# A transformer block on one core: x2's tiles turned into operands stage by stage, low parts of weights emitted later, gate's first sums on VectorE

## The chip, the core and the metric

The kernel runs on one core of one Trainium2 chip. The metric is the device time of one execution in microseconds (us); of several runs the median counts. The engines are named as in the profile: PE (TensorE) multiplies matrices, DVE (VectorE), ACT (ScalarE) and POOL (GpSimd) work on elements, and SP (SyncE) issues the large transfers. Each engine works through its own instructions in the order in which the program emits them, and waits on semaphores for the others. So the order of emission is the schedule.

## The reference, cut to what is computed

One layer of a hybrid decoder block on 512 tokens of width 2048, all in float32:

```python
h = _rms_norm(x, norm1_g)
aq, ak, av, bu, bg, cq, ck, cv = split(h @ w_in)
out_a = _dilated_mixture(rms(aq), rms(ak), av)          # 8 heads x 64, three dilations
out_b = _conformer_conv(bu, bg, conv_w, conv_b, ...)    # 512 channels, 31 taps
out_c = _band_attention(rms(cq), rms(ck), cv, 127, sinks)  # 16 query heads, 2 kv heads
x = x + concat(out_a, out_b, out_c) @ w_out             # "x2" in the kernel
h2 = _rms_norm(x, norm2_g)
x = x + (silu(h2 @ w_gate) * (h2 @ w_up)) @ w_down      # inner width 5632
```

## The kernel before

**Number format.** A float32 product is made of reduced-precision (fp32r) products: each operand is split into a high part, which is the rounded value, and a low part, which is the rest. `mm3` (L244 to L247) does high·high, high·low and low·high for each 128×128 block of weight against 512 tokens. The weight is the stationary operand, the activation the moving one. Activations lie transposed: features on partitions, tokens along the row.

**Weights.** Weights come in units of 128×1024. `pump` issues their loads on SP into raw buffers, `split_up_to` splits them: ScalarE copies the high part wh (L222), VectorE subtracts it for the low part wl (L223). In the FFN ScalarE writes a second copy of the high part, wn, into PSUM (L226), and VectorE subtracts from that (L228). A unit is split two units ahead of its use: `next_unit` emits the split of unit u + 2 and the loads at the start of unit u. There are three buffers each for wh and wl. Some FFN weight tiles are sums of others (`add`, L174, on GpSimd), named 's' and '21' below.

**Order around the change.** The schedule is written out by hand. `Ticks` is a queue: `ticks.after(n, fn, ...)` has fn emitted n ticks later. The projections (`project`) tick after every second of the eight k steps of a unit, the o-projection after every fourth, so a unit of 24 matmuls (eight k steps of three) has two ticks there. During the projections the attention and the convolution are emitted from these ticks, between the matmuls of the projections.

**The o-projection.** Two halves of the contraction, sixteen output tiles n each. Half 0 adds a tile of x to the partial sum (xr, L823) and keeps it in SBUF; half 1 adds the second partial sum (L826), which gives x2[n]. Half 1 goes through n in the order 0, 8, 1, 9, …, 7, 15, so that pairs (j, j + 8) follow one another. In `residual` x2[n] is stored to DRAM on SP, squared and summed into ssum2 for the norm (L343 on ScalarE, L344 on VectorE), and once both tiles of a pair are there `h2_of(j)` makes the operands of the FFN: two scalings (L808, ScalarE), four sums and differences of 256 columns (L813 to L816, VectorE) and seven operands, each a high part by ScalarE (L801) and a low part by VectorE (L802). All of that is emitted in one string at one tick.

**The FFN.** Gate and up products are done as 2×2 blocks with seven products instead of eight, over j = 0 … 7, in the order 5, 1, 7, 6, 2, 4, 3 (called q5, q1, and so on). Each is eight matmuls with high weights over 512 columns (operand's high and low part side by side) and eight with low weights over 256 columns (L916). The first group, g0, starts right after the o-projection. There, q5 and q1 are multiplied for j < 6 first (`EARLY`), then for j = 6 and 7, and then the norm's statistics follow (`norm2a`: matmuls L285, POOL power L352), and after the third product the spread of the norm over the partitions (`norm2b`: transposes L291, ScalarE copies r2b, L880 and L881), both in the bank of the fourth product. `evacs` hold the VectorE reads of a product's bank, emitted after the next product's start.

Of the kernel before, what the change touches and what calls it, by code (L numbers as in the profile page):

```python
# [15 lines left out]
P = 128  # L16
# [93 lines left out]
def kernel(ctx: ExitStack, tc: tile.TileContext, xT, wi, wo, wgu, wd, cst_in, outT):  # L110
# [19 lines left out]
    def slot(name, dt=F32, cols=T):  # L130
        return sp.tile([P, cols], dt, name=name, tag="s")
# [29 lines left out]
    def group(name, m, n, blocks):  # L161

        key = {k: (k, name) for k in ("11", "12", "21", "22", "s")}
        for k in ("21", "22", "11", "12"):
            entries.append((k + "ab"[m] if k == "22" else k, key[k], blocks[k]))
        u = len(works)

        def add(to, a, b, last=None):
            def go():
                if to == a:  # L170
                    out = raws[key[to]][0]
                else:
                    out = take("s" + "ab"[m], key[to], n)
                nc.gpsimd.tensor_add(out[:, :n], raws[key[a]][0][:, :n], raws[key[b]][0][:, :n])  # L174
                if last:
                    drop(key[last])
            return go

        sums[u - 4].append(add("s", "21", "22"))
        sums[u - 3].append(add("21", "21", "11"))  # L180
        sums[u].append(add("s", "s", "11", "11"))
        sums[u + 2].append(add("s", "s", "12"))
        works.extend((key[k], last, None) for k, last in (
            ("s", False), ("11", False), ("21", True), ("s", False), ("12", True), ("22", True), ("s", True)))
# [19 lines left out]
    def pump(limit):  # L204
        while at["entry"] < len(entries) and len(raws) < limit and entries[at["entry"]][0] not in held:
            buf, key, parts = entries[at["entry"]]
            t, o = take(buf, key, sum(p.shape[-1] for p in parts)), 0
            for part in parts:
                nc.sync.dma_start(t[:, o:o + part.shape[-1]], part)
                o += part.shape[-1]  # L210
            at["entry"] += 1

    def split_up_to(i):
        while at["split"] <= min(i, len(works) - 1):
            key, last, eng = works[at["split"]]
            t, n = drop(key) if last else raws[key]
            u = at["split"]
            hi = wp.tile([P, 1024], F32R, name=f"wh{u}", tag="hi", bufs=SPLIT_BUFS)
            lo = wp.tile([P, 1024], F32R, name=f"wl{u}", tag="lo", bufs=SPLIT_BUFS)
            if eng or "high" not in psum:  # L220
                eng = eng or nc.vector
                nc.scalar.copy(hi[:, :n], t[:, :n])  # L222
                eng.tensor_sub(lo[:, :n], t[:, :n], hi[:, :n].bitcast(F32))  # L223
            else:
                near = psum["high"].tile([P, 1024], F32R, name=f"wn{u}", tag="h")
                nc.scalar.copy(near[:, :n], t[:, :n])  # L226
                nc.scalar.copy(hi[:, :n], t[:, :n])
                nc.vector.tensor_sub(lo[:, :n], t[:, :n], near[:, :n].bitcast(F32))  # L228
            splits[u] = (hi, lo)
            at["split"] += 1  # L230
# [5 lines left out]
    def next_unit():  # L236
        sums_now()
        u = at["use"]
        at["use"] += 1
        split_up_to(u + SPLIT_AHEAD)  # L240
        pump(RAW_EARLY if u < 20 else RAW_BUFS)
        return splits.pop(u)

    def mm3(out, wh, wl, xh, xl, start, stop):  # L244
# [142 lines left out]
    def project(name):  # L387
        b = bank(name)
        for half in range(2):
            wh, wl = next_unit()  # L390
            for kk in range(8):
                k = 8 * half + kk
                s = slice(kk * P, (kk + 1) * P)
                mm3(b, wh[:, s], wl[:, s], h_hi[k], h_lo[k], k == 0, k == KT - 1)
                if kk % 2 == 1:
                    ticks.tick()
        return b
# [330 lines left out]
    def split_mix(name):  # L728
        if name not in m_hi:
# [3 lines left out]
            nc.vector.tensor_sub(lo, m, hi.bitcast(F32))  # L733
            m_hi[name], m_lo[name] = hi, lo

    ticks.after(1, spread_r1)
    ticks.after(2, glu, 0, g4[0], g4[1])
    ticks.after(2, glu, 1, g4[2], g4[3])
# [56 lines left out]
    def halves(t):  # L795
        return t[:, :TH], t[:, TH:]

    def operand(q, j, src):
        t = ops[q, j] = slot(f"h{q}_{j}", F32R)
        hi, lo = halves(t)  # L800
        nc.scalar.copy(hi, src)  # L801
        nc.vector.tensor_sub(lo, src, hi.bitcast(F32))  # L802

    def h2_of(j):
        h = []
        for n in (j, j + NJ):
            t = slot(f"h2_{n}")
            nc.scalar.activation(t, x2.pop(n), AF.Copy, scale=col(C_G2 + n))  # L808
            h.append(t)
        (h11, h12), (h21, h22) = halves(h[0]), halves(h[1])  # L810
        ta, tb = slot(f"ta{j}"), slot(f"tb{j}")
        (n1, n3), (n2, n4) = halves(ta), halves(tb)
        nc.vector.tensor_sub(n1, h11, h12)  # L813
        nc.vector.tensor_sub(n3, h12, h22)
        nc.vector.tensor_sub(n2, n3, h11)
        nc.vector.tensor_add(n4, n2, h21)  # L816
        for q, src in ((5, n1), (1, h11), (7, n3), (6, n2), (2, h21), (4, n4), (3, h22)):
            operand(q, j, src)

    def residual(n, b, half):  # L820
        if half == 0:
            t = x2[n] = xr.pop(n)
            nc.vector.tensor_add(t, t, b)  # L823
            return
        t = x2[n]
        nc.vector.tensor_add(t, t, b)  # L826
        nc.sync.dma_start(x2d[n], t)
        add_square(ssum2, t, n, "sr")
        if n >= NJ:
            h2_of(n - NJ)  # L830

    def split_rows(k):
        for name in ROWS[k:k + 3]:
# [6 lines left out]
    for half in range(2):  # L840
        for i, n in enumerate(OUT_ORDER[half]):
            if half == 1 and i == 2:
                ticks.drain()
                b = None
                open_banks(banks=4, high=2)
            b = bank(f"o{half}_{n}")
            wh, wl = next_unit()
            for kk in range(8):
                k = 8 * half + kk
                row = ROWS[k]  # L850
                while row not in m_hi and row not in mix:
                    ticks.tick()
                split_rows(k)
                s = slice(kk * P, (kk + 1) * P)
                mm3(b, wh[:, s], wl[:, s], m_hi[row], m_lo[row], kk == 0, kk == 7)
                if kk % 4 == 3 or i == 0:
                    ticks.tick()
            ticks.after(0, residual, n, b, half)
            if half == 0:
                load_x(i + 2)  # L860
        for row in ROWS[8 * half:8 * half + 8]:
            if half == 0:
                m_hi.pop(row), m_lo.pop(row)
    ticks.drain()
    m_hi = m_lo = r1b = mult_a = bias_a = bias_c = None

    r2b = cp.tile([P, 3 * TH], F32, name="r2b")
# [3 lines left out]
    outs = [bank(f"out{i}") for i in range(4)]  # L873

    def norm2a():
        n2["r"] = token_scale(ssum2, D, "n2", outs[3][:, :NT])[1]

    def norm2b():
        b = spread(n2["r"], "r2s", outs[3])
        nc.scalar.copy(R_12, b)  # L880
        nc.scalar.copy(r2b[:, T:], b[:, :TH])  # L881

# [14 lines left out]
    class Block:  # L897
# [6 lines left out]
            self.banks = dict(zip((5, 1, 7, 6), outs if m == 0 else (outs[3], outs[1], outs[2], outs[0])))  # L904
            self.banks.update({3: self.banks[5], 4: self.banks[7], 2: self.banks[1]})

        def multiply(self, q, w, xs, first=0, last=True):
            wh, wl = w
            b = self.banks[q]
            at = [(x, slice(j * P, (j + 1) * P)) for j, x in enumerate(xs, first)]  # L910

            begin = first == 0 and q in (5, 1, 6, 7)
            for low in ((0, 1) if flip[0] else (1, 0)):
                for x, s in at:
                    out, lhs, rhs = (b[:, TH:], wl, x[:, :TH]) if low else (b, wh, x)
                    nc.tensor.matmul(out, lhs[:, s], rhs, start=begin, stop=last and low == flip[0] and x is xs[-1],  # L916
                                     skip_group_check=True)
                    begin = False
            flip[0] = 1 - flip[0]
            if last:  # L920
                later(0, self.done, q)

        def both(self, q, out):
            nc.vector.tensor_reduce(out, self.banks[q].rearrange("p (a b) -> p b a", a=2),
# [141 lines left out]
            at = LAID.index(q)  # L1066
            nc.sync.dma_start(acts[q, j].bitcast(F32), od[j % NP][:, at * T:(at + 1) * T])

    EARLY = 6
    blk = gate = None  # L1070
    for g in range(2 * NP + len(DOWN)):
        t = g - 2 * NP
# [4 lines left out]
        else:  # L1077
            n, first, end = DOWN[t]
            blk = Down(t)
        early_w = []  # L1080
        for i, q in enumerate(ORDER):
            sums_now()
            run(evacs)
            w = next_unit()
            if g == 0 and i < 2:
                blk.multiply(q, w, [ops[q, j] for j in range(EARLY)], last=False)
                early_w.append((q, w))
                if i == 1:
                    for q, w in early_w:
                        blk.multiply(q, w, [ops[q, j] for j in range(EARLY, NJ)], EARLY)  # L1090
                    norm2a()
            elif t < 0:
                blk.multiply(q, w, [ops[q, j] for j in range(NJ)])
            else:
                blk.multiply(q, w, [acts[q, j] for j in range(first, end)])
            if g == 0 and i == 2:
                norm2b()

            if t == -1:
                for j in range(NJ):  # L1100
# [94 lines left out]
```

## Time and profile before

| what | us |
|---|---|
| median of 3 runs (lowest, highest) | 1935.17 (1934.69, 1935.21) |
| the profiled execution, whole | 1935.7 |
| its span in the trace | 1933.9 |
| PE busy in it | 1902.3 (98%) |
| DVE / ACT / POOL busy | 1471.1 / 1329.0 / 994.1 |
| mean granted TensorE clock | 0.992 |

The profile is of one execution. Its page begins with the busy time of each engine. A view of waits lists for what an engine waited: waiting line, releasing engine and line, microseconds in total, times, and the longest. The timeline lists instructions by start: start in us from the beginning of the span, duration, engine, line, operation, output and inputs, and in brackets the idle time of the engine before it and what ended that. Windows give the busy time of an engine in a stretch (length, busy time, number of instructions), then the TensorE clock that was granted (1.00 is full, 0.50 half), the share of DMA and GB/s. The projections with attention and convolution fill the span up to about 440 us, the o-projection 440 to 620, the FFN the rest.

### The profile page before, as it was taken

Reading aid. Unit: us, or ns where it says so; the run is one execution under the profiler, and the core shown is the slowest. Engines: PE = TensorE matmul, PEld = TensorE weight load, DVE = VectorE, ACT = ScalarE, POOL = GpSimd, SP = SyncE. Lnnn points to the kernel's source line nnn. Section 1 sums busy time; section 2 is a strip of 40 time slices with the busy share of each in tenths; the row PEclk is TensorE's granted clock in tenths of the full one; section 3 lists DMA queues with packets and bytes.
Section 4 is the critical chain, followed back from the end, with each engine's and each line's share of the span. In section 5 each row is a group of like instructions: output and inputs, shape, how many; then the busy total and the mean of one; then the engine's idle time right before and its main releaser. Section 6 shows DMA issues by size and latency. Waiting matters only on the chain.

```text
span 1933.9 us, 29230 instructions
## 1 busy us (share of the span) xinstructions
PE 1902.3 (98%) x10332; PEld 1645.4 (85%) x10332; DVE 1471.1 (76%) x2508; ACT 1329.0 (69%) x1782; POOL 994.1 (51%) x640
## 2 busy tenths in 40 slices
PE   8999999999999999999999999999999999999999
PEld 7888888778877888888888888888888788888888
DVE  6789998997468677777777777777777677767776
ACT  6355654553356888888888888888877577667675
POOL 0111011000001788877887888788876566656564
PEclk9999999989999999999999999999999899999999
DMA  7222222223342344444443544354538987777685
GB/s 263 80 100 67 66 89 75 72 86 115 120 127 80 120 158 165 147 148 169 154 157 135 181 141 171 127 181 145 172 128 294 363 277 277 269 242 272 202 278 194
DMA packets 125651, 319.48 MB, mean 165 GB/s; under 512 B 14016, under 2 KB 29504, under 8 KB 125504
## 3 DMA queue, kind: packets, MB, share of 16 engines
q1 hardware_dynamic: 125360, 317.51, 48.0%
q8 instruction: 81, 1.33, 0.3%
q14 instruction: 66, 0.54, 0.1%
q10 hardware_dynamic: 144, 0.10, 0.0%
HBM read 259.09 MB, written 57.15 MB: 164 GB/s over the span
## 4 chain that ended last, share of the span: by engine, by line
PE 69%; DVE 2%; DMA 1%; ACT 1%; issue 0%; DVEq 0%; SPq 0%; ACTq 0%
PE out L916 66%; PE o L246 1%; PE o L245 1%; DMA a<-od 1%; PE o L247 1%; DVE h L802 0%; DMA od<-u21st 0%; DVE xr L826 0%; DVE wl L223 0%; DVE ssum L344 0%; DVE ta L813 0%; ACT sr L343 0%; ACT h L808 0%; DVE wl L228 0%; ACT wh L222 0%
## 5 line engine op out<-in xcount | busy, mean ns | idle before, releaser
L916 PE MATMUL out<-h,wh 128*128 128x512 f32 x2464 | 590.7, 392 | 3.6 <-DVE h L802 3.6
L916 PEld LDWEIGHTS out<-h,wh 128*128 128x128 f32 x2464 | 454.1, 189 | 91.8 <-DVE h L802 4.1
L916 PEld LDWEIGHTS out<-h,wl 128*128 128x128 f32 x2464 | 316.6, 191 | 13.7 <-ACT r2b L881 1.2
L916 PE MATMUL out<-h,wl 128*128 128x256 f32 x2464 | 320.7, 283 | 1.2 <-ACT r2b L881 1.0
L916 PE MATMUL out<-a,wh 128*128 128x512 f32 x1232 | 300.0, 394 | 3.2 <-DMA a<-od 2.6
L916 PEld LDWEIGHTS out<-a,wh 128*128 128x128 f32 x1232 | 226.9, 189 | 50.5 <-DMA a<-od 3.7
L916 PEld LDWEIGHTS out<-a,wl 128*128 128x128 f32 x1232 | 160.9, 193 | 10.9 <-DMA a<-od 4.4
L916 PE MATMUL out<-a,wl 128*128 128x256 f32 x1232 | 164.8, 285 | 2.4 <-DMA a<-od 2.2
L222 ACT CAST wh<-w 128x1024 fp32r<-128x1024 f32 (+1 forms) x93 | 96.8, 1041 | 98.8 <-PE o L246 33.6
L223 DVE TENSOR_TENSOR wl<-w,wh 128x1024 fp32r<-128x1024 f32 (+1 forms) x93 | 112.5, 1210 | 63.9 <-ACT wh L222 63.6
L929 DVE TENSOR_TENSOR y<-y,out 128x256 f32<-128x256 f32 x120 | 50.6, 421 | 65.5 <-PE out L916 62.4
L422 DVE SCALAR_TENSOR_TENSOR y<-bu,cst,y 128x511 f32<-128x511 f32 (+14 forms) x120 | 87.6, 730 | 0.7
L174 POOL TENSOR_TENSOR w('s', 'g0')_5639<-w('21', 'g0')_5403,w('22', 'g0')_5439 128x1024 f32<-128x1024 f32 x1 | 2.4, 2403 | 116.2 <-DVE wl L223 116.2
L930 DVE TENSOR_TENSOR y<-y,out 128x256 f32<-128x256 f32 x120 | 50.5, 421 | 4.1
L246 PE MATMUL o<-ml_c,wh 128*128 128x512 f32 x128 | 51.0, 399 | 2.2 <-DVE ml_c L733 2.2
L245 PE MATMUL cq<-hh,wh 128*128 128x512 f32 x128 | 51.4, 401 | 1.4 <-DVE mix_c L701 1.4
L245 PE MATMUL o<-mh_c,wh 128*128 128x512 f32 x128 | 52.0, 407 | 0.0
L247 PE MATMUL o<-mh_c,wl 128*128 128x512 f32 x128 | 50.8, 397 | 0.0
L247 PE MATMUL cq<-hh,wl 128*128 128x512 f32 x128 | 50.0, 391 | 0.0
L246 PE MATMUL cq<-hl,wh 128*128 128x512 f32 x128 | 49.9, 390 | 0.0
L245 PE MATMUL in<-hh,wh 128*128 128x512 f32 x64 | 26.1, 408 | 5.2 <-ACT wh L222 5.2
L246 PEld LDWEIGHTS o<-ml_c,wh 128*128 128x128 f32 x128 | 24.6, 192 | 7.3 <-DVE ml_c L733 2.9
(3093 smaller groups left out, 4822.5 us busy)
## 6 DMA issues: line engine op xcount, KB each, us to landing
a<-od SPq DMA_DIRECT2D x196, 256.0 KB, 5.3
w<-in_wi SPq DMA_DIRECT2D x59, 512.0 KB, 3.6
w<-in_wo SPq DMA_DIRECT2D x32, 512.0 KB, 3.6
y<-x2d SPq DMA_DIRECT2D x48, 256.0 KB, 5.4
x2d<-y SPq DMA_DIRECT2D x64, 128.0 KB, 3.4
x<-in_xT SPq DMA_DIRECT2D x16, 256.0 KB, 7.2
xr<-in_xT SPq DMA_DIRECT2D x16, 256.0 KB, 3.9
x2d<-xr SPq DMA_DIRECT2D x16, 256.0 KB, 4.1
```

The costliest lines, as they stand in the source:

```text
L174: nc.gpsimd.tensor_add(out[:, :n], raws[key[a]][0][:, :n], raws[key[b]][0][:, :n])
L222: nc.scalar.copy(hi[:, :n], t[:, :n])
L223: eng.tensor_sub(lo[:, :n], t[:, :n], hi[:, :n].bitcast(F32))
L245: nc.tensor.matmul(out, wh, xh, start=start, stop=False)
L246: nc.tensor.matmul(out, wh, xl, start=False, stop=False)
L247: nc.tensor.matmul(out, wl, xh, start=False, stop=stop)
L422: nc.vector.scalar_tensor_tensor(yconv[j][:, i:], hconv[j][:, :T - i], c, yconv[j][:, i:], op0=ALU.mult, op1=ALU.add)
L916: nc.tensor.matmul(out, lhs[:, s], rhs, start=begin, stop=last and low == flip[0] and x is xs[-1], skip_group_check=True)
L929: sign(out, out if first is None else first, main)
L930: sign(out, out, rest)
```

## The change

Four things move; the arithmetic stays the same.

1. From the start of the attention (`late_lows`) to the end of the o-projection, the subtraction for a weight's low part and the loads by `pump` are emitted at the fourth k step of a unit instead of at its start, ahead of the tick there.
2. x2's tiles become operands in stages one tick apart: `residual`, then `scale_x2` (store and scaling), then `differences` and `square_x2`, then `high`, then `low`. q5's and q1's operands are made from the first tile of a pair alone, one stage ahead of the other five.
3. The early split of q5 and q1 goes: g0's products are multiplied whole. `norm2a` stands after the third product, `norm2b` after the fourth, each in a PSUM tile of the pool "high" that wn uses.
4. The four weight sums of the first gate group 'g0' are emitted on VectorE instead of GpSimd.

```diff
@@ in group(): add()
-                nc.gpsimd.tensor_add(out[:, :n], raws[key[a]][0][:, :n], raws[key[b]][0][:, :n])
+                eng = nc.vector if name == "g0" else nc.gpsimd
+                eng.tensor_add(out[:, :n], raws[key[a]][0][:, :n], raws[key[b]][0][:, :n])
@@ after pump()
+    lows, late_lows = [], []
+
+    def lows_now():
+        while lows:
+            fn, *args = lows.pop(0)
+            fn(*args)
+        if late_lows:
+            pump(RAW_EARLY if at["use"] <= 20 else RAW_BUFS)
@@ in split_up_to()
                 nc.scalar.copy(hi[:, :n], t[:, :n])
-                eng.tensor_sub(lo[:, :n], t[:, :n], hi[:, :n].bitcast(F32))
+                lows.append((eng.tensor_sub, lo[:, :n], t[:, :n], hi[:, :n].bitcast(F32)))
+                if not late_lows:
+                    lows_now()
@@ in next_unit()
+        lows_now()
         split_up_to(u + SPLIT_AHEAD)
-        pump(RAW_EARLY if u < 20 else RAW_BUFS)
+        if not lows:
+            pump(RAW_EARLY if u < 20 else RAW_BUFS)
@@ in project() and, ahead of "if kk % 4 == 3", in the o-projection
+                if kk == 3:
+                    lows_now()
                 if kk % 2 == 1:
                     ticks.tick()
@@ ahead of the attention
+    late_lows.append(True)
     ticks.after(1, spread_r1)
@@ operand(), h2_of() and the old residual() are replaced by
+    half_h = {}
+
+    def residual(n, b, half):
+        t = xr.pop(n) if half == 0 else x2[n]
+        nc.vector.tensor_add(t, t, b)
+        x2[n] = t
+        if half == 1:
+            ticks.after(1, scale_x2, n)
+
+    def scale_x2(n):
+        j = n % NJ
+        t = x2.pop(n)
+        nc.sync.dma_start(x2d[n], t)
+        h = slot(f"h2_{n}")
+        nc.scalar.activation(h, t, AF.Copy, scale=col(C_G2 + n))
+        half_h.setdefault(j, []).append(h)
+        ticks.after(1, differences, j, n)
+        ticks.after(1, square_x2, n, t)
+
+    def square_x2(n, t):
+        if n == 0:
+            nc.scalar.activation(ssum2, t, AF.Square)
+        else:
+            sq = slot(f"sr{n}")
+            nc.scalar.activation(sq, t, AF.Square)
+            ticks.after(1, nc.vector.tensor_add, ssum2, ssum2, sq)
+
+    def differences(j, n):
+        hs = half_h[j]
+        h11, h12 = halves(hs[0])
+        if n < NJ:
+            ta = slot(f"ta{j}")
+            n1, n3 = halves(ta)
+            hs.append(ta)
+            nc.vector.tensor_sub(n1, h11, h12)
+            ticks.after(1, high, j, ((5, n1), (1, h11)))
+            return
+        half_h.pop(j)
+        (n1, n3), (h21, h22) = halves(hs[1]), halves(hs[2])
+        n2, n4 = halves(slot(f"tb{j}"))
+        nc.vector.tensor_sub(n3, h12, h22)
+        nc.vector.tensor_sub(n2, n3, h11)
+        nc.vector.tensor_add(n4, n2, h21)
+        ticks.after(1, high, j, ((7, n3), (6, n2), (2, h21), (4, n4), (3, h22)))
+
+    def high(j, srcs):
+        for q, src in srcs:
+            ops[q, j] = slot(f"h{q}_{j}", F32R)
+            nc.scalar.copy(ops[q, j][:, :TH], src)
+        ticks.after(1, low, j, srcs)
+
+    def low(j, srcs):
+        for q, src in srcs:
+            hi, lo = halves(ops[q, j])
+            nc.vector.tensor_sub(lo, src, hi.bitcast(F32))
@@ after the o-projection
     ticks.drain()
+    lows_now()
+    late_lows.clear()
@@ norm2a, norm2b
-        n2["r"] = token_scale(ssum2, D, "n2", outs[3][:, :NT])[1]
+        b = psum["high"].tile([P, 1024], F32, name="n2b", tag="h")
+        n2["r"] = token_scale(ssum2, D, "n2", b[:, :NT])[1]
-        b = spread(n2["r"], "r2s", outs[3])
+        b = psum["high"].tile([P, 1024], F32, name="r2s", tag="h")[:, :T]
+        spread(n2["r"], "r2s", b)
@@ in the loop over products (multiply() loses its arguments first and last)
-            if g == 0 and i < 2:
-                blk.multiply(q, w, [ops[q, j] for j in range(EARLY)], last=False)
-                early_w.append((q, w))
-                if i == 1:
-                    for q, w in early_w:
-                        blk.multiply(q, w, [ops[q, j] for j in range(EARLY, NJ)], EARLY)
-                    norm2a()
-            elif t < 0:
+            if t < 0:
                 blk.multiply(q, w, [ops[q, j] for j in range(NJ)])
...
-            if g == 0 and i == 2:
-                norm2b()
+            if g == 0 and i in (2, 3):
+                (norm2a if i == 2 else norm2b)()
```

More of the change, by code (lines that the diff above doesn't have):

```diff
@@ L796, in halves @@
         return t[:, :TH], t[:, TH:]
[L798 to L813, printed above, removed]
+    half_h = {}
[34 more added lines that the diff above has]
+        n2, n4 = halves(slot(f"tb{j}"))
         nc.vector.tensor_sub(n3, h12, h22)
@@ L816, in h2_of @@
         nc.vector.tensor_add(n4, n2, h21)
[L817 to L830, printed above, removed]
+        ticks.after(1, high, j, ((7, n3), (6, n2), (2, h21), (4, n4), (3, h22)))
[8 more added lines that the diff above has]
+            nc.vector.tensor_sub(lo, src, hi.bitcast(F32))
     def split_rows(k):
@@ L855 @@
                 mm3(b, wh[:, s], wl[:, s], m_hi[row], m_lo[row], kk == 0, kk == 7)
+                if kk == 3:
+                    lows_now()
                 if kk % 4 == 3 or i == 0:
@@ L865 @@
     m_hi = m_lo = r1b = mult_a = bias_a = bias_c = None
+    lows_now()
+    late_lows.clear()
     r2b = cp.tile([P, 3 * TH], F32, name="r2b")
@@ L905, in __init__, with multiply @@
             self.banks.update({3: self.banks[5], 4: self.banks[7], 2: self.banks[1]})
-        def multiply(self, q, w, xs, first=0, last=True):
+        def multiply(self, q, w, xs):
             wh, wl = w
             b = self.banks[q]
-            at = [(x, slice(j * P, (j + 1) * P)) for j, x in enumerate(xs, first)]
-            begin = first == 0 and q in (5, 1, 6, 7)
+            at = [(x, slice(j * P, (j + 1) * P)) for j, x in enumerate(xs)]
+            begin = q in (5, 1, 6, 7)
             for low in ((0, 1) if flip[0] else (1, 0)):
@@ L915, in multiply @@
                     out, lhs, rhs = (b[:, TH:], wl, x[:, :TH]) if low else (b, wh, x)
-                    nc.tensor.matmul(out, lhs[:, s], rhs, start=begin, stop=last and low == flip[0] and x is xs[-1],
+                    nc.tensor.matmul(out, lhs[:, s], rhs, start=begin, stop=x is xs[-1] and low == flip[0],
                                      skip_group_check=True)
@@ L919, in multiply @@
             flip[0] = 1 - flip[0]
-            if last:
-                later(0, self.done, q)
+            later(0, self.done, q)
         def both(self, q, out):
@@ L1067, in load_act @@
             nc.sync.dma_start(acts[q, j].bitcast(F32), od[j % NP][:, at * T:(at + 1) * T])
-    EARLY = 6
     blk = gate = None
@@ L1079 @@
             blk = Down(t)
-        early_w = []
         for i, q in enumerate(ORDER):
```

## The prediction

> **What bounds the kernel now.** I read the page first, its span and busy time:
>
> ```profile
> span 1933.9 us, 29230 instructions
> PE 1902.3 (98%) x10332; PEld 1645.4 (85%) x10332; DVE 1471.1 (76%) x2508; ACT 1329.0 (69%) x1782; POOL 994.1 (51%) x640
> ```
>
> TensorE is busy for 98%. No matmul is added or removed, so the most that reordering can bring is TensorE's idle time, 1933.9 − 1902.3 = 31.6 us, and what is lost at half clock after a pause. Next the view of waits, TensorE only, from 420 to 640 us (total, times, longest):
>
> ```profile
> PE out L916 <- DVE h L802: 3.6, 1, 3.6
> PE o L246 <- DVE ml_c L733: 2.2, 1, 2.2
> PE a2o L688 <- DVE a2pl L674: 2.0, 2, 1.2
> PE o L246 <- DVE ml_b L733: 1.1, 2, 0.8
> PE out L916 <- ACT r2b L881: 1.0, 1, 1.0
> ```
>
> and from 200 to 235 us:
>
> ```profile
> PE c2o L688 <- DVE c2pl L674: 1.7, 1, 1.7
> PE c7s L611 <- DVE mix_c L701: 0.4, 1, 0.4
> ```
>
> The edits reach the low parts of x2's operands (h, L802), r2b, and the waits for VectorE behind a weight's low part (ml_c, ml_b): 3.6 + 1.0 + 2.2 + 1.1 = 7.9 us at most, plus half clock. The a2pl operands stand behind both the old and the new place of the weight's low part, so that row stays. The clock is read in windows of TensorE (length, busy time, granted clock):
>
> ```profile
> 222.27:225.68 3.41, 1.74 (x12) 1.00 0.29 119
> 420.29:423.70 3.41, 1.44 (x8) 1.00 0.35 133
> 423.70:427.11 3.41, 2.08 (x5) 0.50 0.00 0
> 625.09:628.50 3.41, 0.01 (x1) 1.00 0.21 77
> 628.50:631.91 3.41, 3.41 (x13) 0.50 0.00 0
> 631.91:635.33 3.42, 3.42 (x10) 0.50 0.75 246
> ```
>
> A window with 1.67 us idle (222) is one followed by full clock; one with 1.97 idle (420) and one wholly idle (625) are followed by 0.50. The point lies between, and each window worked through at half clock loses 1.7 us.
>
> **The transition to the FFN, before.** TensorE's timeline around the end of the o-projection (T0 = 619.81):
>
> ```profile
> 618.67 0.39 PE L246 MATMUL o<-ml_a,wh 128*128 128x512 f32 x1
> ...
> 619.81 1.52 PE L916 MATMUL out<-h,wh 128*128 128x512 f32 x6
> ...
> 628.49 0.80 PE L916 MATMUL out<-h,wh 128*128 128x512 f32 x1 [3.65 <-DVE h L802]
> ...
> 638.14 1.21 PE L916 MATMUL out<-h,wl 128*128 128x256 f32 x8 [0.95 <-ACT r2b L881]
> 639.19 3.13 PE L916 MATMUL out<-h,wh 128*128 128x512 f32 x13
> ```
>
> Five matmuls lie between 618.67 and 619.81, a pitch of 0.228 us, so a unit of 24 takes 5.47. The early split lets the products of j < 6, and of j = 6, run first, 628.49 − 3.65 − 619.81 = 5.0 us of work; then TensorE waits 3.65 us for the operands of j = 7 and goes on at half clock for two windows. The fifth product, q2, starts eight matmuls into the last row, at 639.19 + 8 × 0.228 = 641.0, T0 + 21.2. VectorE's timeline shows why the operands are late:
>
> ```profile
> 615.31 1.81 DVE L344 TENSOR_TENSOR ssum<-ssum,sr 128x512 f32<-128x512 f32 x1 [0.70 <-ACT sr L343]
> ...
> 624.15 0.68 DVE L826 TENSOR_TENSOR xr<-xr,o 128x512 f32<-128x512 f32 x1
> ...
> 628.01 0.42 DVE L802 TENSOR_TENSOR h<-ta,h 128x256 fp32r<-128x256 f32 x1
> ...
> 630.36 1.21 DVE L228 TENSOR_TENSOR wl<-w('21', 'g0')_5403,wn 128x1024 fp32r<-128x1024 f32 x1
> ```
>
> x2[15] is made at 624.15, 4.3 us after TensorE finished its sum, behind the string of the pair before; its square, scales, four differences and seven lows follow in one string. Seven lows fill 628.01 to 630.36, 0.34 us each.
>
> **Staging x2 one tick apart (costed as one ring).** In half 1 of the changed kernel one unit is a ring: wl, the lows of the stage before, the differences and xr on VectorE, then scale and the next wh on ScalarE, for which the next wl waits. ScalarE's rows:
>
> ```profile
> 604.40 1.32 ACT L808 ACTIVATE h<-xr,cst 128x512 f32<-128x512 f32 x2
> 605.62 0.39 ACT L801 CAST h<-ta 128x256 fp32r<-128x256 f32 x1
> ...
> 607.90 1.05 ACT L222 CAST wh<-w 128x1024 fp32r<-128x1024 f32 x1
> ```
>
> A unit with five lows and one difference: wl 1.14 (1.21 less the same overlap of 0.08 that the lows have) + 5 × 0.34 + 0.34 + xr 0.68 + scale 0.66 (half of 1.32) + wh 1.05 = 5.57. One with two lows and three dependent differences: 1.14 + 0.68 + 3 × 0.42 + 0.68 + 0.66 + 1.05 = 5.47; five casts run beside the differences and end about with xr. Four hand-overs of some hundredths (my allowance) make both about 5.6. TensorE needs 5.47, so the ring falls back some 0.15 a unit, over eleven units from about 1.2 us (one wl) to 2.9 us behind a unit's start. Squares and ssum lie beside the ring's ScalarE part; if ssum took 1.81 again, that cover would be gone, at up to 1.1 us each time.
>
> The last unit's wl then starts at T0 − 5.47 + 2.9 = 617.2, in the clock of before. wl 1.14, two lows and three differences lead to xr[7] at 620.3; ssum 0.6 and five lows of j = 6 to 623.2; n1 0.34; xr[15] at 623.5, only 0.6 earlier than before's 624.15. But q5's operand of j = 7, cut from x2[7] alone, no longer waits for x2[15]'s string: after xr[15] 0.6 and ssum 0.6 its low ends at 625.2, T0 + 5.4. Against that the filler goes: q5 whole has seven matmuls ahead of that operand, 7 × 0.228 = 1.6 us. TensorE waits 5.4 − 1.6 = 3.8 us, no less than before, but the wait ends at T0 + 5.4 with 4.0 us of q5 and q1 to do instead of at T0 + 8.7 with seven matmuls. One window at half clock adds 1.6, so q1 ends at T0 + 11.0. q7 takes 2.8 (eight matmuls of 0.228 and eight of half the columns), the statistics and the spread 1.3 together (an allowance), q6 2.8, and q2 starts at T0 + 17.9. Gain 21.2 − 17.9 = **3.3 us**. Bounds: 1.6 if half clock lasts two windows as before, 4.9 if none of it comes.
>
> **norm2a and norm2b, one product later, in other banks.** The 0.95 wait for r2b goes, as a whole product (2.8 us) covers the power and spread; it is in the 3.3. Without that cover the 0.95 returns.
>
> **Gate's first sums on VectorE.** Removed from GpSimd:
>
> ```profile
> 614.16 2.42 POOL L174 TENSOR_TENSOR w('s', 'g0')_5639<-w('s', 'g0')_5639,w('11', 'g0')_5506 128x1024 f32<-128x1024 f32 x1 [19.42 <-DVE wl L228]
> ```
>
> While it ran, the ssum at 615.31 took 1.81, against 0.68 for xr of the same shape. Four adds of wl's shape come to VectorE, 4 × 1.21 = 4.8 us. The first two fall where the ring is on ScalarE and end within 0.3 us of the wh that VectorE would wait for; the third stands behind all lows, the fourth behind a wl that is early. Cost between 0 and 2.4 (two uncovered); I take 0.1, inside the ring's 5.6.
>
> **Late low parts, attention.** Each wl, and the SP loads with it, moves behind one to eight VectorE operations. TensorE uses a low part first over 8 us later in the projections (by the order of TensorE's work), so a delay of 2 to 3 us costs nothing; with that slack gone it would be 1.2 a unit. VectorE's order gains only for what stood between the two places. At the ml_c wait, VectorE and then TensorE:
>
> ```profile
> 426.06 1.22 DVE L223 TENSOR_TENSOR wl<-w,wh 128x1024 fp32r<-128x1024 f32 x1
> ...
> 434.85 0.67 DVE L733 TENSOR_TENSOR ml_c<-mix_c,mh_c 128x512 fp32r<-128x512 f32 x1
> ```
>
> ```profile
> 436.32 0.40 PE L246 MATMUL o<-ml_c,wh 128*128 128x512 f32 x1
> ```
>
> This wl goes behind the ml_c that TensorE waits for, which comes 1.14 us sooner. What is late next: the ml_c of 434.85 ends at 435.52, 0.8 before its use, behind work that keeps its place; with what VectorE itself gains, 1.0 to 1.9 can be kept, and I take 1.4. Against it, the wait for mix_c near 220 (0.4) goes, but the c2pl wait behind it takes the time over, and window 222 then has 1.67 + 0.4 = 2.1 us idle, past the point where the clock halved. I set half of a window's 1.7 against the gain: attention net **0.6**, bounds −1 to 2.5.
>
> The Trainium skill, "TensorE: Matmul & The Clock Gate", Part 1: The HAM clock gate, has the clock halve after an idle window of about 3.4 us. Window 420, idle for 1.97 of its 3.41 us, was followed by 0.50 all the same, so the measurement decides; by the rule the 0.8 would fall away.
>
> **ml_b.**
>
> ```profile
> 530.71 1.22 DVE L223 TENSOR_TENSOR wl<-w,wh 128x1024 fp32r<-128x1024 f32 x1 [3.62 <-ACT wh L222]
> ```
>
> VectorE waited 3.62 us for wh with ml_b behind that wl; now ml_b goes first. Of the longer of the two ml_b waits (0.8) **0.65** goes, the rest being for ScalarE's high part; the other stays.
>
> **Sum.** 0.6 + 0.65 + 3.3 = 4.5 us. After 660 the order of every engine is as before. The profiled execution took 1935.7 us around its span of 1933.9, 0.5 above the median of 1935.17; it becomes 1931.2, and the median **1930.7**. A measurement can tell this kernel from no change by about 0.2%, 3.9 us, so the limits are 1931.3 and 1939.0.
>
> **Rivals.**
>
> *Only part arrives.* In attention the next late operation takes the gain down to 1.0 and window 222 turns to half clock (−1.7); the transition keeps 1.6. For it: 3.8 us of wait remain, and 631.91 shows a second half-clock window. Against: nothing stands next behind ml_b. 0.65 + 1.6 + 1.0 − 1.7 = 1.55, so 1933.6.
>
> *Half clock does not come.* If window 222 stays full, and TensorE's wait is cut by a window's edge into parts too short, 0.8 + 1.6 more: 1928.3. For it: how the windows lie against the wait is open. Against: of 3.8 us at least 1.9 lie in one of two windows. The clock page's rule, named above, gives this outcome too.
>
> *The ring is too slow: slower.* If the five casts of every second unit fall into the ring between xr and scale (5 × 0.39 = 1.95, 1.6 with overlap), a unit takes 0.8 more on average, 6.4, and after eleven units j = 7's operand comes 8.8 us later, with 1.6 us of filler where before had 5.0: 1930.7 + 8.8 = 1939.5. It decides from 6.0 us a unit (4.5 / 11 above 5.6), and is slower by over 0.2% from 6.35. For it: the ring has no slack as reckoned. Against: the casts need only the differences, which go ahead of xr.
>
> **How the numbers follow.** Forecast 0.45 (own range 1929.0 to 1932.2), part only 0.33 (1931.3 to 1936), no half clock 0.08, ring 0.14. Faster by over 0.2%: four fifths of the first, and the third, with a little of the second: 0.46. Slower: most of the last: 0.13. Same: 0.41. The range, 1927.2 to 1937.0, leaves out the ring and the lowest of the third case.
>
> **What would show it.** Right: TensorE's wait for h ends 5 to 6 us after the o-projection's last matmul, behind seven matmuls; no wait for r2b; q2 17 to 19 us after T0; xr 2 to 4 us after its unit; no ssum over 0.8 us; the ml_c wait under 1.2; window 222 followed by 0.50 or not. Wrong: that wait ends later than T0 + 8.7, TensorE waits for wl inside the o-projection, or the attention part, up to 525 us, differs by over 2.5 us.

## The result, and the profile after

The changed kernel takes 1930.18 us (median of 13 runs, 1929.51 to 1931.62), the kernel before 1935.21 (13 runs on the same chip): 5.0 us less, a ratio of 0.9976 with an interval of 0.9968 to 0.9983. The forecast was 1930.7, faster.

The page of the changed kernel, span and busy time:

```profile
span 1928.0 us, 29223 instructions
PE 1898.0 (98%) x10332; PEld 1643.8 (85%) x10332; DVE 1469.7 (76%) x2512; ACT 1329.9 (69%) x1782; POOL 985.9 (51%) x636
```

The two profiled executions lie 5.9 us apart, 0.9 more than the medians. Of that, 0.78 stands in the trace by 15 us after the start, where nothing was changed: the clock went to full 1.7 us sooner in this execution (8.98 instead of 10.69 us). It is left out below.

The waits of TensorE after the change, without those for loads and the first weight:

```profile
PE out L966 <- DVE h L873: 3.6, 1, 3.6
PE c2o L706 <- DVE c2pl L692: 3.1, 1, 3.1
PE a2o L706 <- DVE a2pl L692: 2.6, 2, 1.9
PE o L262 <- DVE ml_c L751: 2.4, 3, 1.0
PE bg L261 <- DVE mix_c L719: 1.2, 1, 1.2
PE a0o L706 <- DVE a0pl L692: 0.9, 1, 0.9
PE o L261 <- DVE xr L823: 0.8, 1, 0.8
PE o L262 <- DVE ml_b L751: 0.5, 2, 0.2
PE out L966 <- ACT wh L241: 0.3, 1, 0.3
```

The wait for r2b is gone, ml_b fell from 1.1 to 0.5. The wait for h is as long as before, but ends sooner. TensorE's timeline from the end of the o-projection (T0 = 617.62):

```profile
617.62 1.75 PE L966 MATMUL out<-h,wh 128*128 128x512 f32 x7
623.01 0.50 PE L966 MATMUL out<-h,wh 128*128 128x512 f32 x1 [3.64 <-DVE h L873]
...
635.04 0.60 PE L307 MATMUL r2s<-ident,n2r 128*128 128x128 f32 x4
635.40 2.09 PE L966 MATMUL out<-h,wh 128*128 128x512 f32 x8
```

Seven matmuls, then 3.64 us of waiting, up to T0 + 5.4; q2 starts at 635.40, T0 + 17.8, where it was T0 + 21.2. So the transition gave 3.4 us. Lined up matmul by matmul, 1.4 us more had come by the end of the o-projection, 0.66 of it at ml_b.

VectorE's low parts in half 1 show the ring:

```profile
575.72 1.23 DVE L221 TENSOR_TENSOR wl<-w,wh 128x1024 fp32r<-128x1024 f32 x1 [1.30 <-ACT wh L234]
...
581.31 1.23 DVE L221 TENSOR_TENSOR wl<-w,wh 128x1024 fp32r<-128x1024 f32 x1 [1.15 <-ACT wh L234]
...
586.96 1.23 DVE L221 TENSOR_TENSOR wl<-w,wh 128x1024 fp32r<-128x1024 f32 x1 [1.30 <-ACT wh L234]
...
621.34 0.68 DVE L823 TENSOR_TENSOR xr<-xr,o 128x512 f32<-128x512 f32 x1
```

One unit takes 5.59 and 5.65 us, each wl waits for its wh, and xr[15] is made 3.7 us after T0.

In the attention the sum came out near the forecast, but not its parts. Windows of TensorE after the change:

```profile
221.25:224.02 2.77, 0.28 (x3) 1.00 0.52 180
224.02:227.43 3.41, 2.78 (x10) 0.50 0.02 7
227.43:230.84 3.41, 3.41 (x13) 0.50 0.54 153
418.58:421.99 3.41, 1.46 (x8) 1.00 0.82 263
421.99:425.40 3.41, 2.29 (x5) 0.50 0.12 44
```

The first row is the end of a window that begins at 220.61; all its idle time, 2.5 us, lies there. The c2pl wait is now 3.1 us long and costs two windows at half clock; work that was ahead of the kernel before by 0.8 us at 218 is 2.8 behind at 242. In turn the a0pl wait near 350 fell from 2.0 to 0.9 and its half-clock window went: 3.0 us back. The kernel before had there:

```profile
PE a0o L688 <- DVE a0pl L674: 2.0, 2, 1.8
```

```profile
348.61:352.02 3.41, 1.56 (x8) 1.00 0.46 154
352.02:355.43 3.41, 3.22 (x10) 0.50 0.00 0
```

### The profile page after: what moved, and what is told of

It reads as the page before. It is cut to its first block, busy times and chain, and to the rows that moved or that the text cites. A ratio compares the mean times of both kernels' runs of the same rounds, so it can differ in the third digit from the quotient of the medians.

```text
span 1928.0 us, 29223 instructions
## 1 busy us (share of the span) xinstructions
PE 1898.0 (98%) x10332; PEld 1643.8 (85%) x10332; DVE 1469.7 (76%) x2512; ACT 1329.9 (69%) x1782; POOL 985.9 (51%) x636
## 4 chain that ended last, share of the span: by engine, by line
PE 66%; DMA 1%; DVE 0%; ACT 0%; issue 0%; DVEq 0%; SPq 0%
PE out L966 66%; DMA a<-od 1%; DMA od<-u21st 0%; ACT wn L240 0%; DVE h L873 0%; ACT wh L241 0%; DVE ssum L90 0%; DVE xr L823 0%; PE n2b L301 0%; ACT h L867 0%; ACT h L833 0%; ACT sr L843 0%; PE r2s L307 0%; DVE tb L860 0%; DVE y L978 0%
```

## The experiments

All times are medians against the kernel before, run on the same chip (1934.95 to 1935.58 in the four sets). The theory at the start was that of the prediction: stages and whole products shorten the transition, late low parts help in the attention and at ml_b, the sums on VectorE cost nothing. The rivals were that the parts need each other, and that the sums matter. The intervals are 1.5 to 2.5 us wide to either side, so where two experiments differ by less, the reading rests on the traces.

| kernel | us | against before |
|---|---|---|
| changed kernel | 1930.18 | −5.0 |
| e1, late low parts alone | 1933.40 | −1.65 |
| e8, sums on VectorE alone | 1933.19 | −1.9 |
| e9, both, no stages | 1930.69 | −4.3 |
| e2, changed without late low parts | 1931.67 | −3.4 |
| e3, changed with sums on GpSimd | 1937.28 | +2.2 |
| e4, changed with the early split | 1931.38 | −3.7 |
| e5, last k step in o-projection | 1926.07 | −9.0 |
| e6, last k step in attention | 1928.68 | −6.4 |
| e7, both | 1924.42 | −10.7 |
| e10, e5 with sums on GpSimd | 1927.64 | −7.3 |
| e11, e9 at the last k step | 1928.69 | −6.9 |

**e1, the late low parts alone.** The kernel before with `lows`, `lows_now` and `late_lows` as in the change, and nothing else.

> The kernel before with the first part alone (low parts of weights and their loads at the fourth k step). Theory: the four parts act in separate places, and this one is worth what the trace of the changed kernel shows up to the end of the o-projection without the first 20 us: about 0.7 us in the attention and 0.66 at ml_b, 1.4 together, so 1933.8; the c2pl wait near 221 is about 3.1 us and followed by clock 0.50, the long wait for ml_b is gone, the wait for h at the transition stays 3.6 us and the wait for r2b 1.0. Rival: the low parts and the staging need each other (the ring of half 1), then this kernel gains nothing or loses at the transition: 1935.2 or more.

Measured 1933.40 (ratio 0.9992, 0.9984 to 1.0001; by the times alone that could still be no gain). TensorE's waits up to 545 us are those of the changed kernel, c2pl 3.1 and ml_b 0.5 among them; the wait for h is 3.7, for r2b 0.9, and q2 starts at T0 + 21.2, as in the kernel before. So this part acts by itself and ahead of the transition, as the theory has it.

**e2, the change without them.**

```diff
-    late_lows.append(True)
```

> The changed kernel without its first part (low parts at the unit's start as before, the rest as changed). Theory: the transition keeps its 3.4 us, since in half 1 no tick lies between the two places and VectorE's order is the same; the attention and ml_b go back: 1935.2 - 3.4 = 1931.8; the c2pl wait is again 1.7 with clock 1.00 behind it, ml_b 0.8. Rival: the staging lives on the late low parts; then the wait for h ends later than 5.4 us after the o-projection, and the time is above 1933.

Measured 1931.67 (0.9971 to 0.9989), c2pl 1.7 and ml_b 0.8 (the longer of two) as expected; q2 starts at T0 + 17.8, as in the changed kernel. The transition does not need the late low parts.

**e3, the sums back on GpSimd.**

```diff
-                eng = nc.vector if name == "g0" else nc.gpsimd
+                eng = nc.gpsimd
```

> The changed kernel with gate's first four sums on GpSimd again. Theory: while they run, VectorE's additions with two inputs in SBUF are held up (before: 1.81 instead of 0.68 us for one, 2.6 instead of 0.42 for another, 4.3 us in all); the ring has no slack, so the operands of j = 7 come 2 to 4 us later and the time is 2 to 4 us above the changed kernel's 1930.2: 1932 to 1934. Rival: the hold-up falls where the ring waits for ScalarE, and the four additions of 1.2 us that VectorE is rid of make up for it: 1930.2 or a little less.

Measured 1937.28 (ratio 1.0013, 1.0004 to 1.0022): 7.1 us above the changed kernel and slower than the kernel before. VectorE's timeline, its three longest operations of 256 columns, and TensorE's wait:

```profile
588.17 2.62 DVE L873 TENSOR_TENSOR h<-tb,h 128x256 fp32r<-128x256 f32 x1
590.71 2.61 DVE L873 TENSOR_TENSOR h<-h,h 128x256 fp32r<-128x256 f32 x1
...
615.00 2.62 DVE L873 TENSOR_TENSOR h<-tb,h 128x256 fp32r<-128x256 f32 x1
```

```profile
PE out L966 <- DVE h L873: 9.8, 2, 5.6
```

GpSimd's sum beside the third of them:

```profile
614.89 2.44 POOL L176 TENSOR_TENSOR w('s', 'g0')_5633<-w('s', 'g0')_5633,w('11', 'g0')_5494 128x1024 f32<-128x1024 f32 x1 [21.85 <-DVE wl L242]
```

Each of three low parts took 2.62 instead of 0.42 and ended 0.3 us after GpSimd's sum beside it. 3 × 2.2 = 6.6 us, and xr[15] comes 6.6 us later against T0: nothing of a hold-up is caught up. The theory had the direction right and the size low, since it took the hold-ups of the kernel before (4.3 us). The Trainium skill, "SBUF — State Buffer", section Who interferes with whom, says that a VectorE instruction with two inputs in SBUF contends with a GpSimd instruction that reads SBUF, and that the loser is blocked for the whole of the other's instruction: the 2.62 agrees.

**e4, the early split back.** `multiply` again with `first` and `last`; q5 and q1 for j < 7, then for j = 7.

```diff
+    EARLY = 7
...
+            if g == 0 and i < 2:
+                blk.multiply(q, w, [ops[q, j] for j in range(EARLY)], last=False)
...
```

> The changed kernel with q5 and q1 multiplied for j < 7 first, then for j = 7: 28 matmuls, 4.8 us of work, ahead of the wait for j = 7's operands. Theory: the end of the wait is set by VectorE at 5.4 us after the o-projection, so the wait falls from 3.6 to about 0.6 us and the half clock goes; but q7's high weight is ready only 9.8 us after the o-projection (ScalarE makes it behind the last casts), so that a new wait of about 3.5 us for wh stands ahead of q7, and q2 starts only 1.2 us sooner: 1929.0. Rival: the wait that the filler removes is gained whole, 3 us and the half clock: 1926.6.

Measured 1931.38 (0.9972 to 0.9989), 1.2 us above the changed kernel. TensorE's timeline:

```profile
623.16 0.50 PE L966 MATMUL out<-h,wh 128*128 128x512 f32 x1 [0.40 <-DVE h L873]
...
627.59 3.78 PE L966 MATMUL out<-h,wh 128*128 128x512 f32 x8 [3.46 <-ACT wh L241]
```

The wait for h fell to 0.4, and a wait of 3.46 for q7's wh took its place, both as the theory said. What it forgot is that this wait brings the half clock as well: eight matmuls took 3.78 us instead of 2.0, q2 started at T0 + 19.6 instead of 16.6. As long as q7's wh comes where it does, the filler that the change gives up is no gain.

**e8, the sums on VectorE alone**, in the kernel before.

> The kernel before with the fourth part alone: gate's first four sums on VectorE. Theory: the hold-ups of VectorE by GpSimd go (4.3 us in all, of which a part is caught up in the pauses between strings), four additions of 1.2 us come, two of them in pauses; x2[15] is made 1 to 3 us sooner, so the wait for h falls from 3.6 to 1 to 2.6 us, and a half-clock window may go: 1932 to 1934. That would make the fourth part a large share of the gain at the transition. Rival: without stages VectorE's string has no pause for the additions: 1935.2 or more.

Measured 1933.19 (0.9980 to 0.9998). VectorE and TensorE:

```profile
622.23 0.68 DVE L826 TENSOR_TENSOR xr<-xr,o 128x512 f32<-128x512 f32 x1
```

```profile
626.57 0.50 PE L916 MATMUL out<-h,wh 128*128 128x512 f32 x1 [2.27 <-DVE h L802]
```

T0 is 619.74, so x2[15] is made 2.5 us after it instead of 4.3, and the wait for h falls from 3.65 to 2.27. q2 starts at T0 + 19.4 instead of 21.2.

**e9, late low parts and sums, without stages.** e1 and e8 together; early split and norm as before.

> The kernel before with the first and the fourth part (late low parts at the fourth k step, gate's sums on VectorE), without the stages of x2, with the early split and the norm in its old place. Theory: the two parts alone gave 1.65 and 1.9 us and act in separate places, so they add up: 1935.1 - 3.5 = 1931.5; the rest to the changed kernel's 1930.2, 1.3 us, is then what the stages, the whole products and the norm's new place bring together. Rival: the stages carry the gain at the transition and the sums only serve them: this kernel stays near 1933.4, where the late low parts alone were.

Measured 1930.69 (0.9970 to 0.9988), 0.5 above the changed kernel and 0.8 under the expectation. TensorE (T0 = 617.57):

```profile
634.69 3.82 PE L936 MATMUL out<-h,wh 128*128 128x512 f32 x16
```

q2 starts eight matmuls into this row, at T0 + 19.0: 2.3 us sooner than in e1, 1.2 later than in the changed kernel. With the sums in place, the stages, the whole products and the new place of the norm together bring 0.5 us by the medians and 1.2 in the trace; without the late low parts (e2 against e8) they bring 1.5 to 1.7. So the theory that they carry the transition falls: the sums bring the larger part of its 3.4 us. The two parts gave 4.3 us together and 3.5 apart; in the traces the half clock behind the wait for h lasts one window here and two in e8.

**e5, the ring opened in the o-projection.** One size is changed:

```diff
-                if kk == 3:
+                if kk == 7:
                     lows_now()
                 if kk % 4 == 3 or i == 0:
```

> The changed kernel with one size changed in the o-projection: low parts and loads emitted at the eighth k step of a unit instead of the fourth, behind xr. Theory: the lateness of xr comes from the ring wl - lows - xr - scale - wh - wl of 5.6 us against TensorE's 5.46 a unit; behind xr, wl waits for a wh that was made a unit earlier, so the ring is open and VectorE needs only its own 4.6 us a unit. xr[15] is then made right after TensorE's last matmul (3.7 us sooner), the wait for h falls from 3.6 to under 0.5, no half clock; next late is q7's wh, some 6.3 us after the o-projection with a wait of about 0.8, and q2 starts at 13 to 14 us after it instead of 17.8: 4 to 4.6 us less, 1925.6 to 1926.2. Rival: the lateness is VectorE's sheer work at the end (two strings of lows and the additions), whatever the order; then xr[15] is no sooner and the time stays at 1930.2.

Measured 1926.07 (ratio 0.9951, 0.9939 to 0.9964). VectorE, then TensorE (T0 = 616.63):

```profile
617.88 0.68 DVE L823 TENSOR_TENSOR xr<-xr,o 128x512 f32<-128x512 f32 x1
```

```profile
619.56 0.50 PE L966 MATMUL out<-h,wh 128*128 128x512 f32 x1 [1.18 <-DVE h L873]
...
631.48 2.09 PE L966 MATMUL out<-h,wh 128*128 128x512 f32 x8
```

xr[15] comes 1.25 us after T0 instead of 3.7, the wait is 1.2 without half clock behind it, and q2 starts at T0 + 14.9: 2.9 us from the transition, not 4 to 4.6. In the first half of the o-projection the ml_c waits fell from 2.4 to 0.9 us, which the expectation left out, but the half clock near 421 lasts three windows instead of two; together that is 0.7 us more in the trace. The ring was what made xr late, but with it open xr is still 1.25 us late. The edit moves the loads along with the low parts; the two were not tried apart.

**e10, the open ring with the sums on GpSimd.**

> The kernel with low parts at the eighth k step of the o-projection (1926.1), with gate's first sums on GpSimd again. Theory: in the changed kernel the three hold-ups of 2.2 us each went into the end of the o-projection whole (6.6 us; 7.1 measured), because the ring has no slack; with the ring open VectorE has 5.46 - 4.6 = 0.8 us to spare per unit, so the two hold-ups near 590 (4.4 us, five units ahead of the end) are caught up nearly whole and the third (2.2, one unit ahead) partly: 1.5 to 3 us above 1926.1, 1927.5 to 1929. Rival: a hold-up costs its length wherever it falls: 6.6 us and a half-clock window, 1933 or more.

Measured 1927.64, 1.6 above e5. VectorE (T0 = 616.60):

```profile
620.05 0.68 DVE L823 TENSOR_TENSOR xr<-xr,o 128x512 f32<-128x512 f32 x1
```

Three low parts took 2.62 again, but xr[15] comes 3.5 us after T0, 2.2 later than in e5: the first two hold-ups are caught up, the third is not. A hold-up costs its length only where nothing behind it has slack. Some luck is in the 1.6: the wait for h is 3.4 us, but it lies across two windows, 1.7 us in each, and no half clock followed it.

**e6, the last k step in the attention alone**: the same edit in `project`.

> The changed kernel with the low parts at the eighth k step in the projections and attention alone. Theory: in attention, the operation that TensorE waits for gains 1.14 us wherever the low part goes behind it; at the c2pl wait near 221 the low part now stands behind c2pl, so the wait falls from 3.1 to about 2.0; the a2pl and ml_c waits near 420 may gain 1.1 once. 1.1 to 2.2 us less than the changed kernel, 1.7 more where a half-clock window goes: 1927 to 1929. Rival: VectorE is the bound of attention and every gain is given back at the next wait: 1930.2, with the same sum of waits between 160 and 440 us (about 11 us).

Measured 1928.68 (0.9958 to 0.9981), 1.5 below the changed kernel. TensorE's waits between 150 and 445 us:

```profile
PE o L262 <- DVE ml_c L751: 4.0, 3, 2.7
PE av L261 <- ACT a0e L649: 2.7, 1, 2.7
PE a2o L706 <- DVE a2pl L692: 2.3, 2, 1.5
PE ak0t L548 <- ACT ak0wide L541: 1.0, 1, 1.0
PE bg L261 <- DVE mix_c L719: 0.7, 1, 0.7
```

They add up to 10.7 us, against 10.2 in the changed kernel: the c2pl wait is gone altogether, and a0e, ml_c and ak0t took its time over. On the waits the rival is right. What is gained is the clock: no half-clock window follows 224 any more, where the changed kernel had two. That the 2.7 us wait for a0e brought no half clock in its place hangs on how the windows lay: the longest idle part in one of them was 1.8 us. The profiled execution is the fastest of the six, 0.7 us under the median.

**e7, both**, and the fastest kernel here.

> Both of the two before together: low parts at the eighth k step in attention and in the o-projection. Theory: they act in separate places and add up, 5 to 6.5 us below the changed kernel: 1924 to 1925.5. Rival: they share the split buffers or the loads, which come later too, and TensorE waits for wl or wh inside the o-projection: above the better of the two.

Measured 1924.42 (ratio 0.9945, 0.9933 to 0.9958): 10.7 us below the kernel before and 5.8 below the changed one. The two add up.

**e11, the last k step without stages.**

> As the run with low parts and sums but no stages (1930.7), with the low parts at the eighth k step in attention and o-projection. Theory: the stages pay only when the ring is open. Without them the string of x2[15] (square, scales, differences, lows: 3.9 us to the first low of j = 7) stays whole behind xr[15], so j = 7's operand comes 5.2 us or more after the o-projection, where the staged kernel has it at 2.9; the early split covers most of that, but q7's wh and r2b then come late. The attention gives its 1.5 us: 1927 to 1929.3, 2.5 to 5 us above the staged 1924.4. Rival: the early split serves as well as the stages: 1924.4 to 1926.

Measured 1928.69 (five runs, 1925.87 to 1930.19), on another chip; each against the kernel before on its own chip, it is 3.8 us behind e7. TensorE (T0 = 616.05):

```profile
629.35 0.65 PE L304 MATMUL out<-ident,n2r 128*128 128x128 f32 x4 [2.12 <-POOL n2r L365]
630.95 1.22 PE L936 MATMUL out<-h,wl 128*128 128x256 f32 x8 [0.95 <-ACT r2b L901]
632.00 3.82 PE L936 MATMUL out<-h,wh 128*128 128x512 f32 x16
```

The early split leaves only 1.1 us of waiting for h, but the norm in its old place waits 2.1 for its power and 0.95 for r2b, and q2 starts at T0 + 17.8 against 14.9 in e5. With the ring open, stages, whole products and the norm's later place together are worth 2.9 us in the trace.

## Why the prediction was right, and where it was not

**The transition: right by its own numbers.**

| | forecast | trace |
|---|---|---|
| ring, us a unit | 5.6 | 5.59, 5.65 |
| xr[15] after T0 | 3.7 | 3.7 |
| wait for h | 3.8 | 3.64 |
| its end after T0 | 5.4 | 5.4 |
| windows at half clock | 1 | 1 |
| q2 after T0 | 17.9 | 17.8 |
| gain | 3.3 | 3.4 |

The reckoning went through the changed kernel's orders of VectorE and ScalarE operation by operation, and these came out as written. One window at half clock and not two, worth 1.6 us, was a choice without a row behind it: the kernel before has two there. In that the forecast had luck.

**The gate's sums: the term that was mis-sized.** The prediction put 0.1 us of cost on them and booked the 3.3 under the stages, whose ring already had ssum at its free 0.68. Taken alone, the sums are a gain of 1.9 (e8), and with the stages in place 7.1 (e3). The stages without them are a loss: e1 and e3 differ by the stages, the whole products and the norm's place, and e3 is 3.9 us slower. The bounds that the text set, 0 to 2.4 of cost, left no room for a gain. The row that told it was quoted, 1.81 instead of 0.68; the step that failed was to count what VectorE takes on and not what it is rid of. The total came out all the same, since the ring was reckoned without hold-ups.

**The attention: the sum right by luck, the terms wrong.** Forecast 0.6 net, in the trace 0.75 between 20 and 525 us. The ml_c term (1.4) came to nothing: the wait of 2.2 was split into three of 2.4 together, and the a2pl waits, which were to stay, grew from 2.0 to 2.6. Although the half clock there lasted two windows instead of three, from 418 to 440 nothing was gained. The clock at window 222 was put at half of 1.7; the c2pl wait and its two windows cost 3.6. What balanced it, the a0pl wait with its half-clock window (3.0), does not occur in the prediction. Part of the c2pl wait has a cause that the forecast missed. VectorE, and GpSimd beside it:

```profile
221.01 1.74 DVE L440 SCALAR_TENSOR_TENSOR y<-bu,cst,y 128x488 f32<-128x488 f32 x1
```

```profile
220.19 2.03 POOL L430 TENSOR_TENSOR bu<-bu,bg 128x512 f32<-128x512 f32 x1 [4.39 <-ACT bg L427]
```

The moved operations put this y 0.8 us behind the start of GpSimd's multiply (in the kernel before it started 0.3 us ahead of it and took 0.72), and it took 1.0 us longer than its neighbours of 0.72, ahead of c2pl. That the wait would be shorter without it was not tried by itself.

**ml_b.** Forecast 0.65, in the trace 0.66.

**The clock.** The point between 1.67 and 1.97 us idle held in the windows shown here (1.95 at 418 and 1.85 at 348 were followed by 0.50), and with it the choice to go by the measured windows. As a rule it is too simple. In the kernel before, window 1502.31, idle for only 1.04 us in short waits for loads, was followed by 0.50; in e9 window 623.36 was, idle for 1.19, with eight one-column matmuls of the norm counted as busy. What decides is open.

**The rivals.** "Half clock does not come" did not happen: 224 and 623 show it. "The ring is too slow" is what e3 is: 1937.3, by hold-ups of 6.6 us and not by the casts. "Only part arrives" fits the attention, where the c2pl wait brought the half clock and the gain at ml_c did not arrive, but not the transition, which kept 3.4 us and not 1.6.

**Still open:** why TensorE's waits between 150 and 445 us add up to nearly the same in the kernel before, the changed one and e6 (10.1, 10.2 and 10.7 us), while the single ones differ. That VectorE is the bound there would give this; no run took work away from it.

## What to carry to other kernels

When two engines hand work to and fro once per step, add up the whole round with its hand-overs and set it against the step of the bounding engine: 5.6 against 5.46 looked like nothing and made the last operand late by 3.7 us, and moving one operation behind the other by four k steps opened the ring and was worth 4.1 us more, nearly as much as the whole change (5.0). In such a ring look for operations that take longer than their kind: every hold-up arrives at the end in full, so work that goes to a less busy engine can cost more than it frees. And price a removal as carefully as an addition.

## What was not expected of the hardware

A VectorE operation of 0.42 us with both inputs in SBUF took 2.62 beside a GpSimd sum of 1024 columns (2.44 to 2.77), each of the six times that it happened in e3 and e10; in the kernel before the same collision cost 1.1 on an ssum that started 1.2 us into the sum. And the half clock followed windows that were idle for only 1.85 to 1.97 of 3.41 us, and in the kernel before one idle for 1.04, while a wait of 3.4 us across two windows (e10, 1.7 us in each) brought none. Once there, it lasted two windows after the c2pl wait and one after the wait for h.
